# A float32 decoder trunk on one core: attention scores and causal pooling from float32r parts, the mask added by VectorE, and small matmul steps lined up

## The chip, the cores and the metric

The kernel runs on one core of a Trainium2 chip. The metric is the device time in microseconds (us) of one execution; lower is better. Beside the time, one execution is recorded by the hardware profiler; its engines are called PE (TensorE matmuls), PEld (TensorE weight loads), DVE (VectorE), ACT (ScalarE), POOL (GpSimd) and SP (SyncE, which starts the transfers here).

## The reference

Two layers over 256 tokens of width 1024. Each layer is a half-step SwiGLU, a mixer, and a second half-step SwiGLU, every one behind an RMS norm whose scale and shift come from a conditioning vector. The mixer of layer 0 is the even one, that of layer 1 the odd one.

```
def even_mixer(h, w_in, w_pool, pool_scale, lam_params, subln_g, w_out, lambda_init):
    p = h @ w_in                                  # u: 4 groups of 128; q, k: 4 heads x 2 x 64; v: 4 x 128
    y_pool = pool_mixer(u, w_pool, pool_scale)
    y_diff = diff_attention(q, k, v, lam_params, subln_g, lambda_init)
    return concatenate([y_pool, y_diff]) @ w_out

def pool_mixer(u, w_group, scale):                # group g: window w = 2, 4, 8, 16
    total = cumsum(u)[t] - cumsum(u)[t - w]
    pooled = total / min(t + 1, w) - u
    return (pooled_g @ w_group[g]) * scale

def diff_attention(...):                          # per head, c = 0 and 1
    s_c = q_c k_c^T (64 wide), causal mask, p_c = softmax(s_c / 8)
    o = rmsnorm((p_0 - lam * p_1) @ v) * subln_g * (1 - lambda_init)
```

The odd mixer is a chunkwise mLSTM with two chunks of 128 tokens and four heads: gates, a running maximum, scores, a carried state, a norm per head.

## The kernel before

Everything is kept transposed: a tile holds 128 features (partitions) by 256 tokens. A *unit* is one 128x128 block of a trunk weight against a 256-column input. Weights (`raww`) stream in chunks of 1 MB; each half chunk of 8 units is cut by ACT (L288, `wh`) and DVE (L289, `wl`) into two float32r parts whose sum is the float32 weight, and the input is likewise `xh` and `xl`. A unit is then three float32r matmuls (`mm3`, lines L330, L331, L332): wh·xh, wl·xh, wh·xl. Modulation weights (`rawm`) stream beside them; DVE reduces each half chunk in one custom instruction (L256).

What is not a unit is written as Python generators, called lanes: `head(h)` (scores, softmax, values, norm), `turn_v`, `pool_group` and, in the odd mixer, `gates`, `head_qk`, `head_v`. A lane issues its small matmuls, then yields a number of units after which it goes on. The emitted program then goes through a list scheduler, and the order of each engine is what comes out of it; each engine runs its instructions in that order. PSUM has 8 banks, each `one()` is a bank. Small float32 matmuls go to PE as two records each, float32r ones as one record.

In the first half step (`first_ffn`) the inputs of k tile 0 to 7 are made one after another: `xn[k]` (x times rstd, L518: DVE for k = 0, POOL for k = 1 to 7), `xh` (ACT L548), a second copy in float32 (ACT L549), `xl` (DVE L550), behind the modulation columns of that k (`acol`, L356). 48 matmuls (`START_BLOCKS`) use each k before the next is needed. `constants()` is written behind that loop, but its POOL instructions, which wait for nothing, are placed early by the scheduler: the four 128x384 matrices `band` (L220 to L229) by which the pooling is a matmul.

In the even mixer `head` adds the mask by a matmul (L616: identity times `masks3`, 384 columns, 128 rows) and then the product of q and k on the 64 rows of one half of the array (L618, L620, float32), for c = 0 and c = 1. `pool_group` multiplies u by `w_pool` (L686, two float32 matmuls) and the result by a band (L691, L692, L693, three). The block order is q, k, v of head 0 to 3 and then u3, u2, u1, u0, so the pooling stands at the end; `EVEN_OUT_K` is the order in which the output projection takes the eight parts of the mixer's result (0 to 3 pooling, 4 to 7 heads).

In `gates` of the odd mixer four float32 matmuls with 4 rows (L798) spread a row over the partitions, one for each head, 6 units apart.

## Time and profile before

| | |
|---|---|
| time, median of 3 runs | 1001.25 us (1001.18 to 1003.7) |
| span of the profiled execution | 1000.4 us |
| busy share PE / DVE / ACT / POOL | 97% / 79% / 53% / 19% |
| matmul instructions | 8004 |
| mean DMA rate | 247 GB/s |

The span is that of one profiled execution; the median of the runs lies 0.85 us above it. The times of matmuls overlap (one is shown as 0.28 us long where the next begins 0.12 us later), so distances between starts are to be read, not lengths. Idle time of an engine that nothing waits for costs nothing.

### The profile page before, as it was taken

How to read it: one execution, taken by the hardware profiler on the slowest of the kernel's cores; microseconds unless marked ns; L12 is line 12 of the kernel's file. 1: busy time of each engine (PE TensorE's matmuls, PEld its weight loads, DVE VectorE, ACT ScalarE, POOL GpSimd, SP SyncE). 2: the span in 40 equal slices, each digit the busy share in tenths (PEclk: the TensorE clock that was granted, in tenths of full speed). 3: DMA queues.
4: the chain of work that ended last, by engine and by line, in shares of the span. 5: the costliest groups of instructions: out<-in, count | busy, mean ns of one | idle time of the engine just before them, and what ended most of it. 6: DMA issues, size and time to landing. Idle time of an engine off the chain costs nothing.

```text
span 1000.4 us, 19729 instructions
## 1 busy us (share of the span) xinstructions
PE 973.0 (97%) x8004; PEld 959.4 (96%) x8004; DVE 788.0 (79%) x1362; ACT 527.5 (53%) x838; POOL 192.1 (19%) x219
## 2 busy tenths in 40 slices
PE   5899999999999999999999999999999999999996
PEld 3899999998999999999999999999999999999996
DVE  5889998978878888887778888787767987777452
ACT  4466444447666445544455555444767664455441
POOL 7314220010112222211122222000000122222011
PEclk9999999999999999999999999999999999999998
DMA  8888888977647667677766767777545766564531
GB/s 339 275 333 296 334 329 312 345 284 268 223 156 275 253 238 268 252 247 259 273 232 253 257 249 253 259 292 290 212 170 213 257 234 221 194 231 173 180 112 43
DMA packets 36382, 247.18 MB, mean 247 GB/s; under 512 B 4033, under 2 KB 4417, under 8 KB 7746
## 3 DMA queue, kind: packets, MB, share of 16 engines
q1 hardware_dynamic: 36290, 245.92, 67.4%
q8 instruction: 62, 1.02, 0.4%
q14 instruction: 30, 0.25, 0.1%
HBM read 244.86 MB, written 1.05 MB: 246 GB/s over the span
## 4 chain that ended last, share of the span: by engine, by line
PE 87%; DVE 5%; issue 3%; POOL 2%; ACT 2%; DMA 1%; SPq 0%; DVEq 0%; POOLq 0%; ACTq 0%
PE one L330 28%; PE one L332 28%; PE one L331 28%; DVE wl L289 2%; DMA xa<-xT 1%; DVE rawm L256 1%; ACT wh L288 1%; POOL hr L398 1%; POOL band L229 0%; DVE xl L389 0%; PE one L620 0%; PE one L618 0%; POOL band L225 0%; PE one L415 0%; PE one L407 0%
## 5 line engine op out<-in xcount | busy, mean ns | idle before, releaser
L330 PE MATMUL one<-xh,wh 128*128 128x258 f32 (+1 forms) x1728 | 491.0, 286 | 4.3 <-ACT xh L548 4.3
L332 PE MATMUL one<-xl,wh 128*128 128x258 f32 (+1 forms) x1728 | 486.6, 284 | 3.1 <-DVE xl L550 2.9
L331 PE MATMUL one<-xh,wl 128*128 128x258 f32 (+1 forms) x1728 | 485.3, 283 | 0.5 <-DVE wl L289 0.5
L288 ACT ACTIVATE wh<-raww 128x1024 fp32r<-128x1024 f32 x320 | 337.8, 1058 | 273.6 <-PE one L332 244.0
L289 DVE TENSOR_TENSOR wl<-raww,wh 128x1024 fp32r<-128x1024 f32 x320 | 393.1, 1230 | 105.2 <-ACT wh L288 100.0
L330 PEld LDWEIGHTS one<-xh,wh 128*128 128x128 f32 x1728 | 328.4, 191 | 7.6 <-ACT xh L548 4.8
L331 PEld LDWEIGHTS one<-xh,wl 128*128 128x128 f32 x1728 | 328.7, 191 | 1.1 <-DVE wl L289 0.9
L332 PEld LDWEIGHTS one<-xl,wh 128*128 128x128 f32 x1728 | 325.7, 190 | 3.8 <-DVE xl L550 3.2
L330 PE MATMUL one<-hid,wh 128*128 128x256 f32 x832 | 234.2, 282 | 0.5 <-ACT hid L563 0.5
L332 PE MATMUL one<-hid,wh 128*128 128x256 f32 x832 | 233.6, 281 | 0.0
L331 PE MATMUL one<-hid,wl 128*128 128x256 f32 x832 | 233.2, 280 | 0.0
L475 POOL TENSOR_TENSOR hid<-h,hid 128x256 fp32r<-128x256 f32 x88 | 116.0, 1319 | 379.2 <-ACT hid L474 379.2
L256 DVE CUSTOM_DVE_ANT_0 rawm<-rawm,cact 128x1024 f32<-128x1024 f32 x144 | 188.2, 1335 | 0.0
L330 PEld LDWEIGHTS one<-hid,wh 128*128 128x128 f32 x832 | 156.7, 188 | 0.8 <-ACT hid L563 0.8
L331 PEld LDWEIGHTS one<-hid,wl 128*128 128x128 f32 x832 | 157.2, 189 | 0.0
L332 PEld LDWEIGHTS one<-hid,wh 128*128 128x128 f32 x832 | 156.6, 188 | 0.2 <-DVE hid L564 0.2
L382 POOL TENSOR_TENSOR acc<-acc,sq 128x256 f32<-128x256 f32 x41 | 34.5, 841 | 270.4 <-ACT sq L378 270.2
L489 DVE TENSOR_TENSOR t<-one,rext 128x258 f32<-128x258 f32 x132 | 55.2, 421 | 30.8 <-PE one L332 30.1
L470 ACT ACTIVATE sg<-t 128x256 f32<-128x256 f32 x66 | 33.0, 504 | 34.4 <-DVE t L489 33.3
L474 ACT ACTIVATE hid<-h 128x256 fp32r<-128x256 f32 x88 | 36.7, 417 | 21.5 <-DVE h L472 21.3
L472 DVE SCALAR_TENSOR_TENSOR h<-t,sg 128x256 f32<-128x256 f32 x66 | 32.4, 491 | 6.9 <-ACT sg L470 0.6
L441 DVE SCALAR_TENSOR_TENSOR xa<-one,gcol,xa 128x256 f32<-128x256 f32 x48 | 22.3, 478 | 17.1 <-PE one L332 17.1
(211 smaller groups left out, 479.6 us busy)
## 6 DMA issues: line engine op xcount, KB each, us to landing
raww<-wst SPq DMA_DIRECT2D x152, 1024.0 KB, 4.9
rawm<-mst SPq DMA_DIRECT2D x71, 1024.0 KB, 5.0
raww<-wst SPq DMA_DIRECT2D x16, 512.0 KB, 7.0
xa<-xT SPq DMA_DIRECT2D x4, 256.0 KB, 4.0
rawm<-mst SPq DMA_DIRECT2D x2, 512.0 KB, 8.7
outT<-fin SPq DMA_DIRECT2D x3, 256.0 KB, 2.8
pk<-pack SPq DMA_DIRECT2D x1, 416.0 KB, 6.6
outT<-fin SPq DMA_DIRECT2D x2, 128.0 KB, 2.7
```

The lines of the kernel that those rows point to most:

```text
L256: nc.vector.tensor_tensor_reduce(out=ri, in0=ri, in1=cact, scale=1.0, scalar=0.0, op0=ALU.mult, op1=ALU.add, accum_out=modc[n // KT][:, n ...
L288: nc.scalar.activation(whs[i], src, AF.Copy)
L289: ins = nc.vector.tensor_tensor(out=wls[i], in0=src, in1=whs[i].bitcast(F32), op=ALU.subtract)
L330: nc.tensor.matmul(out, lhsT=wh, rhs=rh, start=start, stop=False, skip_group_check=skip)
L331: nc.tensor.matmul(out, lhsT=wl, rhs=rh, start=False, stop=False, skip_group_check=skip)
L332: nc.tensor.matmul(out, lhsT=wh, rhs=rl, start=False, stop=stop, skip_group_check=skip)
L382: eng.tensor_tensor(out=stat["acc"], in0=stat["acc"], in1=sq, op=ALU.add)
L470: nc.scalar.activation(sg, gate, AF.Silu, bias=bias_g)
L472: nc.vector.scalar_tensor_tensor(out=h, in0=up, scalar=bias_u, in1=sg, op0=ALU.add, op1=ALU.mult)
L474: nc.scalar.activation(hh[:, 0:T], h, AF.Copy)
L475: nc.gpsimd.tensor_tensor(out=hl[:, 0:T], in0=h, in1=hh[:, 0:T].bitcast(F32), op=ALU.subtract)
L489: nc.vector.tensor_tensor(out=t[:, i, :], in0=ts.pop((f, i))[:, 0:XC], in1=rext, op=ALU.mult)
```

## The change

Scores: q and k are kept as two float32r parts each; a head's scores are 12 float32r matmuls on 64 rows that take c = 0 and c = 1 in turn, and the mask is added by DVE in the instruction that finds the row maximum; the exponential reads the sum from SBUF. Pooling: the window sums are made by POOL as shifted adds (1, 2, 3 and 4 of them for windows 2, 4, 8 and 16), the mean minus the token by DVE, and one product with `w_pool` is left, as three float32r matmuls. The bands go, 16 small constants and the two parts of `w_pool` come. `meet` rounds the place of a lane's next step up to a grid of 12 units. The four L798 matmuls of the odd mixer are issued together. The pooling parts are used in another order by the output projection. Comments in code were removed, which moves line numbers (L288/L289 become L281/L282, L256 becomes L249; L330 to L332 stay).

```diff
-EVEN_OUT_K = (4, 5, 6, 3, 2, 7, 1, 0)
+EVEN_OUT_K = (4, 5, 6, 3, 2, 1, 0, 7)
...
-        for g, w in enumerate(WINDOWS):
-            nc.gpsimd.memset(band[:, g, :], 1.0 / w)
...
-                nc.gpsimd.tensor_tensor(out=m[:, 0:P], in0=m[:, 0:P], in1=ident, op=ALU.subtract)
+        for t in range(PAD):
+            nc.gpsimd.memset(icnt[:, t:t + 1], 1.0 / (t + 1))
...
+        nc.vector.tensor_copy(wph, pcol("w_pool", 0, 512))
+        nc.vector.tensor_tensor(out=wpl, in0=pcol("w_pool", 0, 512), in1=wph.bitcast(F32), op=ALU.subtract)
...
+    def meet(n):
+        to = unit_next[0] + n - grid[0]
+        return grid[0] + -(-to // grid[1]) * grid[1] - unit_next[0]
...
         def head(h):
-            yield 8
+            yield 6
...
-            for c in range(2):
-                rows = slice(64 * c, 64 * c + 64)
-                nc.tensor.matmul(pp[c][:, 0:3 * P], lhsT=identr, rhs=masks3, start=True, stop=False,
-                                 skip_group_check=True)
-                nc.tensor.matmul(pp[c][:, 0:P], lhsT=q[rows, 0:P], rhs=kk[rows, 0:P], start=False, stop=True,
-                                 skip_group_check=True)
-                nc.tensor.matmul(pp[c][:, P:3 * P], lhsT=q[rows, P:T], rhs=kk[rows, 0:T], start=False, stop=True,
-                                 skip_group_check=True)
+            for to, qs, ks in ((slice(0, P), slice(0, P), slice(0, P)), (slice(P, 3 * P), slice(P, T), slice(0, T))):
+                for j, (a, b) in enumerate(((0, 0), (1, 0), (0, 1))):
+                    for c in range(2):
+                        rows = slice(64 * c, 64 * c + 64)
+                        nc.tensor.matmul(pp[c][:, to], lhsT=q[a][rows, qs], rhs=kk[b][rows, ks], start=j == 0,
+                                         stop=j == 2, skip_group_check=True)
...
-                    nc.vector.tensor_reduce(out=mx[:, i, c:c + 1], in_=pp[c][:, cols[i]], axis=AX.X, op=ALU.max)
+                    nc.vector.tensor_tensor_reduce(
+                        out=sc[:, c, cols[i]], in0=pp[c][:, cols[i]], in1=masks3[:, cols[i]], scale=1.0, scalar=NEG,
+                        op0=ALU.add, op1=ALU.max, accum_out=mx[:, i, c:c + 1])
...
         def pool_group(g, src, bias):
...
+            while d < w:
+                n = tmp.tile([P, PAD + T], F32, tag="ps", name=nm("ps"))
+                lo = 2 * d - 1
+                nc.gpsimd.tensor_tensor(out=n[:, lo:PAD + T], in0=s[:, lo:PAD + T], in1=s[:, lo - d:PAD + T - d],
+                                        op=ALU.add)
+                s, d = n, 2 * d
             z = slot()
-            nc.scalar.activation(z[:, 0:T], pz[:, 0:T], AF.Copy)
-            yield 18
+            nc.vector.scalar_tensor_tensor(out=z[:, 0:T], in0=s[:, PAD:PAD + T], scalar=1.0 / w,
+                                           in1=u[:, PAD:PAD + T], op0=ALU.mult, op1=ALU.subtract)
+            e = z[:, 0:w - 1]
+            nc.vector.tensor_tensor(out=e, in0=s[:, PAD:PAD + w - 1], in1=icnt[:, 0:w - 1], op=ALU.mult)
+            nc.vector.tensor_tensor(out=e, in0=e, in1=u[:, PAD:PAD + w - 1], op=ALU.subtract)
+            zh, zl = slot(F32R), slot(F32R)
+            nc.scalar.activation(zh[:, 0:T], z[:, 0:T], AF.Copy)
+            nc.vector.tensor_tensor(out=zl[:, 0:T], in0=z[:, 0:T], in1=zh[:, 0:T].bitcast(F32), op=ALU.subtract)
+            yield 12 + 2 * g
             ps = one()
-            nc.tensor.matmul(ps[:, 0:P], lhsT=z[:, 0:P], rhs=band[:, g, 0:P], start=True, stop=True)
-            nc.tensor.matmul(ps[:, P:T], lhsT=z[:, 0:P], rhs=band[:, g, P:T], start=True, stop=False)
-            nc.tensor.matmul(ps[:, P:T], lhsT=z[:, P:T], rhs=band[:, g, T:3 * P], start=False, stop=True)
+            sl = slice(g * P, (g + 1) * P)
+            for j, (a, b) in enumerate(((wph, zh), (wpl, zh), (wph, zl))):
+                nc.tensor.matmul(ps[:, 0:T], lhsT=a[:, sl], rhs=b[:, 0:T], start=j == 0, stop=j == 2)
...
+            ph, pl = slot(F32R), slot(F32R)
+            nc.scalar.activation(ph[:, 0:T], src, AF.Identity, bias=bias)
+            nc.vector.scalar_tensor_tensor(out=pl[:, 0:T], in0=src, scalar=bias, in1=ph[:, 0:T].bitcast(F32),
+                                           op0=ALU.add, op1=ALU.subtract)
+            parts[blk] = (ph, pl)
...
+            pbs = [one(), one()]
             for h in range(NH):
-                pb4 = one()
-                nc.tensor.matmul(pb4[:, 0:T], lhsT=ident[0:4, h:h + 1].broadcast_to([4, P]), rhs=mr,
-                                 start=True, stop=True)
+                nc.tensor.matmul(pbs[h // 2][:, (h % 2) * T:(h % 2 + 1) * T],
+                                 lhsT=ident[0:4, h:h + 1].broadcast_to([4, P]), rhs=mr, start=True, stop=True)
```

POOL at the start, before: these are the rows around the norm's `nr` (L398) and the first of the seven `xn` adds (L518, output `hid`); the band of the last window is still ahead of them.

```order
L398 TENSOR_TENSOR nr_185<-nv_183,mhalf 128x2
L229 TENSOR_TENSOR band<-band,ident 128x128 x2
L220 MEMSET band 128x384 x2
L222 MEMSET band 128x1 x7
L225 AFFINE_SELECT band<-band 128x128
L225 AFFINE_SELECT band<-band 128x256
L227 AFFINE_SELECT band<-band 128x128
L227 AFFINE_SELECT band<-band 128x256
L229 TENSOR_TENSOR band<-band,ident 128x128 x2
```

The rows that follow are 15 memsets and the same steps for the other window, and then the L518 rows. With the change, POOL at the same place:

```order
L220 MEMSET icnt 128x1 x16
L683 MEMSET pu_3349 128x16
L683 MEMSET pu_3401 128x16
L398 TENSOR_TENSOR nr_186<-nv_184,mhalf 128x2
L518 TENSOR_TENSOR hid_194<-xa,rext 128x256
L518 TENSOR_TENSOR hid_196<-xa,rext 128x256
L518 TENSOR_TENSOR hid_198<-xa,rext 128x256
```

Between `nr` and the first L518 nothing is left. On PE, the scores of head 0 before (the names `one` are PSUM banks, `hid` are q and k):

```order
L332 MATMUL one_2797<-xl_96,wh_2707 128x258
L616 MATMUL one_2822<-masks_121,identr 128x384
L618 MATMUL one_2822<-hid_2779,hid_2775 128x128
L620 MATMUL one_2822<-hid_2779,hid_2775 128x256
L616 MATMUL one_2823<-masks_121,identr 128x384
L618 MATMUL one_2823<-hid_2779,hid_2775 128x128
L620 MATMUL one_2823<-hid_2779,hid_2775 128x256
L330 MATMUL one_2797<-xh_89,wh_2707 128x258
```

With the change, the same head on PE (L618 are now all score matmuls, the two banks are c = 0 and c = 1):

```order
L618 MATMUL one_2782<-hid_2743,hid_2738 128x128
L618 MATMUL one_2783<-hid_2743,hid_2738 128x128
L330 MATMUL one_2763<-xh_90,wh_2669 128x258
L331 MATMUL one_2763<-xh_90,wl_2670 128x258
L332 MATMUL one_2763<-xl_98,wh_2669 128x258
L618 MATMUL one_2782<-hid_2744,hid_2737 128x128
L618 MATMUL one_2783<-hid_2744,hid_2737 128x128
L618 MATMUL one_2782<-hid_2743,hid_2737 128x256
L618 MATMUL one_2783<-hid_2743,hid_2737 128x256
```

The two banks alternate, and one unit of the trunk stands in the middle; heads 1 and 2 have such a unit too. On DVE, where the last blocks of the input projection come in, the order with the change is this (L579 is the block's first step, L693 to L700 the pooling of group 3 and then 2, L282 and L249 the weight part and the modulation sum):

```order
L579 TENSOR_TENSOR ti_3465<-one_3418,rext 128x258
L249 ISA rawm_3419,mod_110<-rawm_3419,cact 128x1024
L249 ISA mod_110 128x1
L700 TENSOR_TENSOR hid_3365<-hid_3360,hid_3364 128x256
L693 SCALAR_TENSOR_TENSOR hid_3410<-ps_3408,pu_3401 128x256
L282 TENSOR_TENSOR wl_3553<-raww_3550,wh_3552 128x1024
L696 TENSOR_TENSOR hid_3410<-ps_3408,icnt 128x7
L579 TENSOR_TENSOR ti_3534<-one_3482,rext 128x258
L697 TENSOR_TENSOR hid_3410<-hid_3410,pu_3401 128x7
L282 TENSOR_TENSOR wl_3620<-raww_3550,wh_3619 128x1024
L700 TENSOR_TENSOR hid_3415<-hid_3410,hid_3414 128x256
L693 SCALAR_TENSOR_TENSOR hid_3474<-ps_3472,pu_3467 128x256
```

PE's order just behind the last block, with the change (L705 are the pooling matmuls, L330 to L332 with `hid` inputs the output projection):

```order
L332 MATMUL one_3482<-xl_98,wh_3369 128x258
L666 MATMUL one_3509<-ident,hid_3432 128x128 x2
L643 MATMUL one_3516<-ident,sc_3265 128x128 x3
L705 MATMUL one_3556<-hid_3414,wph 128x256
L705 MATMUL one_3556<-hid_3414,wpl 128x256
L705 MATMUL one_3556<-hid_3415,wph 128x256
L330 MATMUL one_3549<-hid_3215,wh_3423 128x256
L331 MATMUL one_3549<-hid_3215,wl_3424 128x256
```

`hid_3415`, the last of the pooling inputs that PE takes ahead of the output projection, is written by DVE's next to last row above.

## Rows read from the trace of the kernel before

**Rows 1.** The page's first part: busy time, share of the span and instructions of each engine.

```profile
PE 973.0 (97%) x8004; PEld 959.4 (96%) x8004; DVE 788.0 (79%) x1362; ACT 527.5 (53%) x838; POOL 192.1 (19%) x219
```

**Rows 2.** Busy time by stretch (window, its length; then busy us and count of PE, PEld, DVE, ACT, POOL; granted clock; DMA share; GB/s): the end of the even mixer's input projection.

```profile
226.00:284.00 58.00, 57.44 (x441) 52.87 (x440) 47.51 (x130) 40.77 (x111) 4.58 (x4) 1.00 0.66 245
```

**Rows 3.** PE's timeline in the first half step (start, length, engine, line, operation, xcount, [idle before <- what ended it]).

```profile
26.44 0.28 PE L332 MATMUL one<-xl,wh 128*128 128x256 f32 x1
...
27.48 0.28 PE L331 MATMUL one<-xh,wl 128*128 128x256 f32 x1
30.62 0.58 PE L332 MATMUL one<-xl,wh 128*128 128x256 f32 x1 [2.87 <-DVE xl L550]
...
33.57 0.31 PE L330 MATMUL one<-xh,wh 128*128 128x256 f32 x1
```

**Rows 4.** POOL's timeline of the same time, in the same columns.

```profile
13.39 2.63 POOL L229 TENSOR_TENSOR band<-band,ident 128x128 f32<-128x128 f32 x2
...
25.84 6.99 POOL L518 TENSOR_TENSOR hid<-xa,rext 128x256 f32<-128x256 f32 x7
```

**Rows 5.** ACT's timeline: rstd spread over the tokens (`rext`, which the adds of L518 read), and the first row that waits for such an add.

```profile
14.74 0.38 ACT L514 ACTIVATE rext<-one 128x256 f32<-128x256 f32 x1 [3.34 <-PE one L415]
...
26.60 0.60 ACT L548 ACTIVATE xh<-hid,bcol,acol 128x256 fp32r<-128x256 f32 x1 [6.28 <-POOL hid L518]
```

**Rows 6.** DVE's timeline: the modulation columns (`acol`) of k tiles 1 and 2, the parts `xl` of k tiles 1, 2 and 3, and a modulation sum between.

```profile
22.48 0.31 DVE L356 SCALAR_TENSOR_TENSOR acol<-sc,pk 128x1 f32<-128x1 f32 x1
...
29.63 0.94 DVE L550 TENSOR_TENSOR xl<-hid,xh 128x256 fp32r<-128x256 f32 x1
30.49 1.74 DVE L256 CUSTOM_DVE_ANT_0 rawm<-rawm,cact 128x1024 f32<-128x1024 f32 x1
...
34.15 0.16 DVE L356 SCALAR_TENSOR_TENSOR acol<-sc,pk 128x1 f32<-128x1 f32 x1
...
37.13 0.42 DVE L550 TENSOR_TENSOR xl<-hid,xh 128x256 fp32r<-128x256 f32 x1
...
43.05 0.42 DVE L550 TENSOR_TENSOR xl<-hid,xh 128x256 fp32r<-128x256 f32 x1
```

**Rows 7.** PE's timeline where the first blocks of the first half step are finished.

```profile
71.62 0.28 PE L330 MATMUL one<-xh,wh 128*128 128x256 f32 x1
72.14 0.39 PE L331 MATMUL one<-xh,wl 128*128 128x256 f32 x1 [0.24 <-DVE wl L289]
```

**Rows 8.** ACT's timeline just before: two loads of function tables.

```profile
66.06 1.28 ACT L603 ACT_TABLE_LOAD   x1
...
67.93 1.28 ACT L470 ACT_TABLE_LOAD   x1
```

**Rows 9.** PE's timeline at the scores of head 0, from the last trunk matmul ahead to the second one behind.

```profile
225.92 0.28 PE L332 MATMUL one<-xl,wh 128*128 128x258 f32 x1
226.04 0.34 PE L616 MATMUL one<-masks,identr 128*128 128x384 f32 x1
...
226.63 0.60 PE L620 MATMUL one<-hid,hid 64*128 64x256 f32 x2
...
228.60 0.28 PE L331 MATMUL one<-xh,wl 128*128 128x258 f32 x1
```

**Rows 10.** The weight loads of the same time, behind the scores.

```profile
228.37 0.19 PEld L330 LDWEIGHTS one<-xh,wh 128*128 128x128 f32 x1 [0.33 <-issue]
228.48 0.19 PEld L331 LDWEIGHTS one<-xh,wl 128*128 128x128 f32 x1
```

**Rows 11.** PE's timeline at the end of the even mixer's input projection: band products of two groups, the `w_pool` products of two, and a wait in the output projection.

```profile
278.66 0.39 PE L691 MATMUL one<-band,hid 128*128 128x128 f32 x2
...
280.81 0.36 PE L330 MATMUL one<-hid,wh 128*128 128x256 f32 x1
...
281.13 0.28 PE L332 MATMUL one<-hid,wh 128*128 128x256 f32 x1
281.96 0.39 PE L330 MATMUL one<-hid,wh 128*128 128x256 f32 x1 [0.54 <-ACT hid L563]
```

**Rows 12.** PE's timeline at one of the four L798 steps of the odd mixer.

```profile
720.03 0.28 PE L332 MATMUL one<-xl,wh 128*128 128x258 f32 x1
720.24 0.69 PE L798 MATMUL one<-mr,ident 4*128 4x256 f32 x2
...
721.09 0.29 PE L331 MATMUL one<-xh,wl 128*128 128x258 f32 x1
```

**Rows 13.** DVE's groups of instructions in 226 to 284 us (line, operation, shapes, xcount, then busy us, mean ns of one, idle before and its releasers).

```profile
L289 DVE TENSOR_TENSOR wl<-raww,wh 128x1024 fp32r<-128x1024 f32 x14 | 17.1, 1218 | 1.5 <-ACT wh L288 1.4
L256 DVE CUSTOM_DVE_ANT_0 rawm<-rawm,cact 128x1024 f32<-128x1024 f32 x11 | 13.1, 1215 | 0.0
L579 DVE TENSOR_TENSOR ti<-one,rext 128x258 f32<-128x258 f32 x14 | 5.9, 423 | 3.8 <-PE one L332 3.8
L627 DVE TENSOR_REDUCE mx<-one 128x1 f32<-128x256 f32 x8 | 3.2, 415 | 0.0
...
L564 DVE SCALAR_TENSOR_TENSOR hid<-one,gc,hid 128x256 fp32r<-128x256 f32 x4 | 1.9, 482 | 1.4 <-ACT hid L563 1.4
```

**Rows 14.** POOL's groups of the whole span, in the same columns.

```profile
L475 POOL TENSOR_TENSOR hid<-h,hid 128x256 fp32r<-128x256 f32 x88 | 116.0, 1319 | 379.2 <-ACT hid L474 379.2
L382 POOL TENSOR_TENSOR acc<-acc,sq 128x256 f32<-128x256 f32 x41 | 34.5, 841 | 270.4 <-ACT sq L378 270.2
```

More of the change, by code (lines that the diff above doesn't have):

```diff
@@ L176, in trunk_kernel @@
     modc = [const.tile([P, KT], F32, name=f"mod{g}") for g in range(DEPTH * NSUB * 3)]
-    masks3 = const.tile([P, 3 * P], F32R, name="masks3")
-    identr = const.tile([P, P], F32R, name="identr")
+    masks3 = const.tile([P, 3 * P], F32, name="masks3")
     maskT = const.tile([P, P], F32, name="maskT")
     tri = const.tile([P, P], F32, name="tri")
-    band = const.tile([P, len(WINDOWS), 3 * P], F32, name="band")
+    icnt = const.tile([P, PAD], F32, name="icnt")
+    wph = const.tile([P, 512], F32R, name="wph")
+    wpl = const.tile([P, 512], F32R, name="wpl")
     wgh = const.tile([P, 64], F32R, name="wgh")
@@ L205, in constants @@
     def constants():
[L206 to L207 removed]
+        nc.gpsimd.memset(masks3, 0.0)
         for i in (0, 2):
[L209 removed]
+            m = masks3[:, i * P:(i + 1) * P]
+            nc.gpsimd.affine_select(out=m, in_=m, pattern=[[-1, P]],
                                     compare_op=ALU.is_ge, fill=NEG, base=0, channel_multiplier=1)
[L211 to L212 removed]
         nc.gpsimd.memset(maskT, 0.0)
@@ L309, in tick @@
                 step(lane)
+    grid = [0, 1]
+    def meet(n):
+        to = unit_next[0] + n - grid[0]
+        return grid[0] + -(-to // grid[1]) * grid[1] - unit_next[0]
     def run_until(cond):
@@ L669, in turn_v @@
         def turn_v(i):
[L670 removed]
+            yield meet(4)
             p = parts.pop(("v", i))
@@ L676, in turn_v @@
             nc.scalar.activation(v[:, 0:T], pt[:, 0:T], AF.Copy)
-            yield 9
             vT[i] = v
         def pool_group(g, src, bias):
-            u = keep(src, bias)
-            yield 16
-            pz = one()
-            for i in range(2):
-                sl = slice(i * P, (i + 1) * P)
-                nc.tensor.matmul(pz[:, sl], lhsT=u[:, sl], rhs=pcol("w_pool", g * P, P), start=True, stop=True)
-            z = slot()
-            nc.scalar.activation(z[:, 0:T], pz[:, 0:T], AF.Copy)
@@ L689, in pool_group @@
-            yield 18
+            w = WINDOWS[g]
+            u = tmp.tile([P, PAD + T], F32, tag="pu", name=nm("pu"))
+            nc.gpsimd.memset(u[:, 0:PAD], 0.0)
+            nc.scalar.activation(u[:, PAD:PAD + T], src, AF.Identity, bias=bias)
+            s, d = u, 1
+            while d < w:
[4 more added lines that the diff above has]
+                s, d = n, 2 * d
@@ L709, in rhs @@
             return ys[k]
+        grid[:] = [unit_next[0] + 4, 12]
         in_proj(EVEN_IN_ORDER, scalars, done)
@@ L906, in rhs @@
             return ys[k]
+        grid[:] = [unit_next[0], 12]
         in_proj(ODD_IN_ORDER, lambda: spawn(gates()), done)
```

56 lines of the change are left out of this document (22 added, 34 removed).

## The prediction

> **What bounds the kernel now.** I read the busy shares first: PE is busy 97% of the span and DVE 79% [rows 1]. PE's timeline then shows what its time is made of: one trunk matmul starts 0.12 us after the other (225.92 to 226.04 in [rows 9]), and it leaves that rhythm only for small matmuls, or where an input is late. So a change gains by what it takes from PE's row of work or from PE's waits, and loses by what it makes PE wait for. Three places matter. At the start PE stands still for a vector result at 27.48 [rows 3], and the chain behind it ends on POOL, which is busy with the bands until 25.84 [rows 4]. In the even mixer the scores of a head take 2.44 us of PE (225.92 to 228.60 less two trunk steps of 0.12, [rows 9]). At the end of that mixer's input projection DVE is busy 47.51 of 58 us [rows 2]: it follows PE at 82%, and whatever is put on it there has some 10 us of room.
>
> **The change part by part.** All terms are against the profiled span of 1000.4 us; the median of the runs lies 0.85 us above it.
>
> *Start, -4.3 us.* POOL's bands go. The seven adds L518 (7.0 us, [rows 4]) can begin when `rext` is there at 15.1 [rows 5] and are done near 22, not 32.8. ACT's `xh` of k tile 1 then no longer waits 6.28 us for an add [rows 5] but for its modulation column, which was there at 22.8 [rows 6]. The adds now run beside DVE's work of 15 to 22 us; such company makes a modulation sum 1.74 us instead of 1.22 ([rows 6] against the mean of [rows 13]), so I put the column about 0.7 us later, at 23.5. From the column to the end of `xl` an undisturbed k tile takes 3.2 us (34.31 to 37.55 for k tile 2, [rows 6]), so PE gets k tile 1 at about 27 instead of 30.6. From there a k tile costs DVE and ACT 5.92 us (37.13 to 43.05, [rows 6]), which makes k tile 2 ready at 32.9 to 33.2 where it was 37.5. PE's own work on a k tile is 48 x 0.12 = 5.7, less than that, so PE follows this chain up to k tile 7 and keeps the whole shift: -4.3. Part of it is the 13 matmuls from 30.62 to 33.57 at half speed, 2.95 us instead of 1.55 [rows 3], behind the stop. Bounds: -5.3 if the column isn't late at all, -3.3 if the adds delay it by 1.7.
>
> *Table loads, -0.4 us.* The two loads of 1.28 us stand ahead of the first activations of the SwiGLU [rows 8], and PE waits 0.40 us more than a step at 71.62 [rows 7]. In the new order these activations come first. DVE gets the two parts of `w_pool` near here, about 1.2 us, so I don't count more; bounds 0 and -0.85.
>
> *Scores, -1.5 us.* 12 float32r matmuls replace 2 mask products and 4 float32 products. The trace has no float32r matmul on 64 rows. Those with 256 columns can't go faster in one queue than 0.12 each, those with 128 columns not faster than their weight load, 0.11 (228.37 to 228.48, [rows 10]): 6 x 0.12 + 6 x 0.11 = 1.37. Leaving and re-entering full height costs 0.39: the four records of an L798 step need 4 x 0.108 at full clock and take 0.82 (720.03 to 721.09 less two steps, [rows 12]). A head is 1.76, and three heads have a trunk unit in the middle, which pays the 0.39 again. 4 x 1.76 + 3 x 0.4 = 8.3 against 9.8 now: -1.5. Bounds: if the halves c = 0 and c = 1 run beside each other the 1.37 becomes 0.69, -4.2 in all; if each of the 11 changes of half within a head costs like a change of height on one side, 0.195, it is +7.1. I take no cost for a change of half and no overlap, the middle.
>
> *Pooling on PE, -2.9 us.* Two groups' bands and two groups' `w_pool` products take 2.15 us (278.66 to 280.81, [rows 11]), so four groups 4.3. Twelve float32r matmuls of 256 columns take 1.4.
>
> *Odd mixer, -1.2 us.* Four steps of L798 pay the change of height four times, now once: 3 x 0.39. PE has no other wait there that would take it back; the results come earlier for heads 1 to 3. The grid of 12 units puts other small float32 products together, but those have all 128 rows and pay no change of height; I count 0 for it, +-0.5.
>
> *DVE at the end of the even mixer, +5 us.* New on DVE: the low parts of q and k, 8 x 0.48; the mask added with the row maximum, which by the custom instruction's 1.2 us for 1024 columns costs what the reduction costs (0.42 for 256) and a read of 0.08; for each pooling group 0.48 + 0.43 and two short ones, 1.2 ([rows 13] for all of these). That is 3.9 + 1.3 + 4.8 = 10 us in a stretch with 10 to spare, and the pooling part comes at its very end, in the same few blocks. There I followed DVE's order from the first step of block u3 to the result that the output projection takes third (head 2): four weight parts (4.9), three modulation sums (3.9), three block steps (1.3), the end of head 3's softmax (1.6), three pooling groups (3.6), three parts of results (1.4) and some twenty short ones (2), about 18.7 us, and some 1.5 us of contention, since ten shifted adds of at least 0.84 us [rows 14] run on POOL. PE's row between the same points is three blocks of 24 matmuls (8.6), the output projection's first nine (1.1), and the small products: 14.8. DVE is 5.4 us behind, in waits at L705 and at the output projection's third and fifth inputs. Today's wait there is 0.7 (281.13 to 281.96, [rows 11]); the adds' own chain for window 16, 4 x 0.84 to 1.32, makes the first `z` late by a little more. Net +5. Bounds: +1 if the waits of DVE overlap as they do now, +8 if each add costs 1.3 and blocks the DVE step beside it.
>
> The Trainium skill (SBUF — State Buffer, "Who interferes with whom") has only the port pair shared by VectorE and GpSimd as a cause of contention, and as an exclusive lock. By full blocking the ten adds would cost DVE up to 8 us there rather than my 1.5; the trace's 1.74 against 1.22 is a loss of 0.5 in an instruction, less than a whole add.
>
> Sum: -4.3 - 0.4 - 1.5 - 2.9 - 1.2 + 5.0 = -5.3, a span of 995.1 and a time of 996.0.
>
> **The rivals.**
>
> *The halves overlap.* Consecutive score matmuls use different rows of the array and different banks. Then the scores gain 2.7 more: 993.3. Nothing in the trace shows two halves one behind the other (now a mask product of full height lies between them). The Trainium skill (TensorEngine Tiling (Array Packing), "Key Properties") says that different tiles can load and multiply in parallel, and that only a change of tiling mode, not of tile, drains the array. Our 0.39 at a change of height agrees with the second; for the first no row speaks.
>
> *Each change of half drains* (the other side). With a price p of a change, the scores cost 44 p more. At p = 0.12 the whole gain is gone, from 0.19 on the kernel is slower by over 3 us; at the 0.195 that a change of height costs on one side it is +8.6: 1004.6. For it speaks that every change of rows in the trace costs this; against it that none of them keeps the height.
>
> *The start gains nothing.* If DVE or the transfers, and not the adds, set when the early k tiles are ready, the 4.3 stays: 1000.3. Against it stands the named releaser in [rows 5].
>
> *DVE's end takes less or more.* At +1 the time is 992, at +8 999; only from +13 on would it be slower.
>
> **How the numbers follow.** The sum as it stands, with the end between its bounds: 0.50. Overlap 0.20. No gain at the start 0.12. Changes of half that drain 0.09; a worse end of the even mixer than +8, 0.09. 0.3% (3 us) is what a measurement can tell from no change. Faster: the first, the second and a part of the rest, 0.71; within 3 us: 0.18; slower: 0.11. The likeliest case's own range is 992 to 999. The range of 8 in 10 goes from 990 (overlap with a small end) to 1001.5 (no gain at the start with a larger end, or half of the draining).
>
> **What would show it.** In the trace after: no band on POOL, L518 from about 15 us, PE's k tile 1 without the 2.9 us wait, k tile 2 at 33; a head's scores 1.8 us (2.2 with a unit in the middle), and from their starts whether two halves begin together (overlap), 0.11 to 0.12 apart (as summed) or 0.3 apart (drain); one L798 group of 1.3 us; at 270 to 285 us waits of PE on DVE at L705 and L330 of 5 to 6 us together. I am wrong if PE has no waits there, or if the early shift is gone by 72 us.

## The result and the profile after

The changed kernel takes 1013.5 us (median of 4 runs, 1012.4 to 1013.9) where the kernel before takes 1001.5 (median of 4): a ratio of 1.0114 [1.0102, 1.0126], slower by 1.1%. The forecast was 996.0 with a range of 990 to 1001.5. The profiled execution has a span of 1012.2 us, 11.8 longer than before.

The page's first part of the changed kernel, which answers to [rows 1]:

```profile
span 1012.2 us, 19704 instructions
PE 970.5 (96%) x7984; PEld 958.6 (95%) x7984; DVE 800.2 (79%) x1402; ACT 529.2 (52%) x838; POOL 182.6 (18%) x195
```

PE has 20 instructions and 2.5 us of busy time less, and the span is longer: the time went into waits, and into stretches at half clock. Both kernels have the same 7680 trunk matmuls, in the same order but for the parts of the even mixer's output projection, so the start of the n-th in one trace can be set against the n-th of the other. The lag of the changed kernel (negative: it is earlier) is: -2.1 us at k tile 2 of the first half step (n = 96; 35.38 against 37.47), -1.4 at 78 us, +4.7 behind the even mixer (n = 2208), +4.2 ahead of the odd mixer's heads (n = 5424), +11.9 behind them (n = 6144). So the start gave 1.4, the even mixer took 6.2 and the odd mixer 7.7.

**The start.** POOL, DVE and PE of the changed kernel (start, length, ..., [idle before <- what ended it]), to be set beside [rows 3 to 6]:

```profile
13.32 1.78 POOL L398 TENSOR_TENSOR nr<-nv,mhalf 128x2 f32<-128x2 f32 x1 [9.72 <-DMA raww<-wst]
16.88 9.29 POOL L518 TENSOR_TENSOR hid<-xa,rext 128x256 f32<-128x256 f32 x7 [1.78 <-ACT rext L514]
```

```profile
13.33 1.22 DVE L249 CUSTOM_DVE_ANT_0 rawm<-rawm,cact 128x1024 f32<-128x1024 f32 x1
...
22.15 1.75 DVE L249 CUSTOM_DVE_ANT_0 rawm<-rawm,cact 128x1024 f32<-128x1024 f32 x1
...
25.51 0.68 DVE L353 TENSOR_TENSOR bcol<-mod,pk 128x1 f32<-128x1 f32 x1
...
26.30 0.16 DVE L356 SCALAR_TENSOR_TENSOR acol<-sc,pk 128x1 f32<-128x1 f32 x1
...
29.28 0.42 DVE L550 TENSOR_TENSOR xl<-hid,xh 128x256 fp32r<-128x256 f32 x1
```

```profile
29.75 0.39 PE L332 MATMUL one<-xl,wh 128*128 128x256 f32 x1 [0.30 <-DVE xl L550]
```

The 2.87 us wait of [rows 3] is 0.30 now, as forecast. But POOL's `nr` on two columns takes 1.78 us: it starts at 13.32, DVE's modulation sum at 13.33, and `nr` ends 0.6 us behind that sum's end (14.55). In the run with late bands below the order is nearly the same, and it takes 0.70:

```profile
13.26 0.70 POOL L399 TENSOR_TENSOR nr<-nv,mhalf 128x2 f32<-128x2 f32 x1 [10.28 <-DMA raww<-wst]
```

```profile
13.29 1.25 DVE L257 CUSTOM_DVE_ANT_0 rawm<-rawm,cact 128x1024 f32<-128x1024 f32 x1
```

The 17 traces of this document split in the same way. In four of them `nr` begins between 0.004 us ahead of a modulation sum and 0.04 us behind its start; there it takes 1.74 to 1.78 and ends 0.55 to 0.56 behind the sum. In the other 13 it begins 0.02 us or more ahead of the sum and takes 0.70 to 0.72.

The seven adds take 9.29 us instead of 7.0, and three of DVE's short steps take 0.68 or 0.69 instead of 0.15. The column of k tile 1 is there at 26.46, not 23.5. Some 0.6 us of this isn't the change's: `nr` starts at 13.32 where it started at 12.72 before, and over the 17 traces, whatever the kernel, it starts at 11.76 to 13.32.

**The end of the even mixer.** ACT, DVE and PE, where before there was one wait of 0.54 us [rows 11]:

```profile
273.81 0.42 ACT L699 ACTIVATE hid<-hid 128x256 fp32r<-128x256 f32 x1 [2.37 <-DVE hid L697]
...
277.34 1.06 ACT L281 ACTIVATE wh<-raww 128x1024 fp32r<-128x1024 f32 x1 [2.63 <-PE one L332]
278.69 0.42 ACT L699 ACTIVATE hid<-hid 128x256 fp32r<-128x256 f32 x1 [0.29 <-DVE hid L697]
...
279.41 0.26 ACT L657 ACTIVATE hid<-one 128x128 f32<-128x128 f32 x1
...
281.80 0.63 ACT L661 ACTIVATE hid<-one,hr 128x128 f32<-128x128 f32 x2 [1.78 <-POOL hr L398]
```

```profile
273.19 0.59 DVE L697 TENSOR_TENSOR hid<-hid,pu 128x15 f32<-128x15 f32 x1
...
280.83 0.15 DVE L396 TENSOR_SCALAR hv<-ss 128x2 f32<-128x2 f32 x1
```

```profile
274.28 0.39 PE L705 MATMUL one<-hid,wph 128*128 128x256 f32 x1 [2.39 <-ACT hid L699]
...
282.22 0.73 PE L666 MATMUL one<-ident,hid 128*128 128x128 f32 x2 [4.91 <-ACT hid L661]
```

The longest wait of PE isn't for a pooling product. L666 transposes the result of head 2, whose values PE had finished at 267.4. Its squares (L657) stand on ACT behind two pooling parts (L699), each waiting for DVE, and run at 279.4. They stand behind a weight part (L281) too, which waits 2.63 us for PE's own matmuls, so a delay of PE comes back to it through ACT. The clock falls behind the first wait (columns as in [rows 2], 4 us each):

```profile
270.00:274.00 4.00, 1.89 (x16) 1.67 (x15) 3.97 (x7) 1.26 (x2) 2.54 (x3) 1.00 0.31 68
274.00:278.00 4.00, 3.03 (x14) 2.73 (x14) 4.00 (x8) 1.37 (x3) 1.67 (x3) 0.59 0.84 307
278.00:282.00 4.00, 0.00 (x0) 0.00 (x0) 4.00 (x22) 1.93 (x8) 2.08 (x4) 0.50 0.71 231
282.00:286.00 4.00, 3.78 (x21) 3.67 (x22) 3.08 (x21) 2.73 (x8) 0.00 (x0) 0.63 0.49 207
```

From about 274.8 to 285 the granted clock is at half: trunk matmuls there start 0.215 us apart instead of 0.12. DVE is busy without a gap from 270 to 282, while PE is busy for 4.9 of these 12 us.

**The scores.** Head 3 on PE, to be set beside [rows 9] (x8 are eight matmuls in one row):

```profile
256.68 0.44 PE L618 MATMUL one<-hid,hid 64*128 64x128 f32 x4
257.49 0.73 PE L618 MATMUL one<-hid,hid 64*128 64x128 f32 x8 [0.37 <-DVE hid L719]
258.15 0.39 PE L330 MATMUL one<-xh,wh 128*128 128x258 f32 x1
258.38 0.28 PE L331 MATMUL one<-xh,wl 128*128 128x258 f32 x1
```

The single records start in pairs: 256.682 and 256.686, 256.846 and 256.849, 257.492 and 257.495, 257.657 and 257.661, 257.829 and 257.832, 257.946 and 257.949. The two halves of the array work beside each other, at 0.12 to 0.17 us a pair where none waits. Counted as in the prediction (and with head 0's end taken like the others', since a transpose follows it), the four heads take 2.05, 1.86, 1.82 and 1.66 us, 7.4 in all, with 1.6 of waiting for low parts in them; before it was 4 x 2.44 = 9.8.

**The odd mixer.** PE's waits there (us in total, times, longest); before it had 1.2 us in all:

```profile
PE one L890 <- ACT hid L885: 3.3, 1, 3.3
PE one L865 <- ACT hid L846: 1.5, 2, 1.0
PE one L844 <- DVE hid L842: 0.9, 3, 0.5
PE one L865 <- ACT dr L876: 0.3, 1, 0.3
```

The longest is at the other end from the first heads: L890 transposes the result of the last head, and between trunk matmuls 5900 and 5920 the lag grows from 6.9 to 12.3.

```profile
786.92 0.48 PE L890 MATMUL one<-ident,hid 128*128 128x128 f32 x1 [3.27 <-ACT hid L885]
```

The scale that this head's squares (L880, ACT) need is ready on DVE at 777.05; they run at 782.50, behind steps of other blocks.

### The profile page after: what moved, and what is told of

Its sections match the earlier page's. It is cut to its first block, busy times and chain, and to the rows that moved or that the text cites. A ratio compares the mean times of both kernels' runs of the same rounds, so it can differ in the third digit from the quotient of the medians.

```text
span 1012.2 us, 19704 instructions
## 1 busy us (share of the span) xinstructions
PE 970.5 (96%) x7984; PEld 958.6 (95%) x7984; DVE 800.2 (79%) x1402; ACT 529.2 (52%) x838; POOL 182.6 (18%) x195
## 4 chain that ended last, share of the span: by engine, by line
PE 85%; DVE 6%; issue 4%; ACT 3%; POOL 1%; DMA 1%; SPq 1%; DVEq 0%; ACTq 0%; POOLq 0%
PE one L330 28%; PE one L332 27%; PE one L331 27%; DVE wl L282 2%; DVE rawm L249 1%; ACT wh L281 1%; DMA raww<-wst 1%; DVE xl L389 1%; PE one L415 0%; POOL ps L689 0%; POOL hr L398 0%; ACT sc L631 0%; DVE sc L625 0%; DVE ti L579 0%; POOL nr L398 0%
## 5 line engine op out<-in xcount | busy, mean ns | idle before, releaser
L330 PE MATMUL one<-xh,wh 128*128 128x258 f32 (+1 forms) x1728 | 489.7, 285 | 4.5 <-ACT xh L548 4.5
L332 PE MATMUL one<-xl,wh 128*128 128x258 f32 (+1 forms) x1728 | 486.6, 284 | 0.6 <-DVE xl L550 0.5
L281 ACT ACTIVATE wh<-raww 128x1024 fp32r<-128x1024 f32 x320 | 337.6, 1058 | 280.9 <-PE one L332 253.3
L282 DVE TENSOR_TENSOR wl<-raww,wh 128x1024 fp32r<-128x1024 f32 x320 | 395.6, 1239 | 104.7 <-ACT wh L281 99.5
L330 PEld LDWEIGHTS one<-xh,wh 128*128 128x128 f32 x1728 | 328.8, 191 | 5.6 <-ACT xh L548 4.8
L332 PEld LDWEIGHTS one<-xl,wh 128*128 128x128 f32 x1728 | 325.8, 190 | 1.5 <-DVE xl L550 1.0
L330 PE MATMUL one<-hid,wh 128*128 128x256 f32 x832 | 234.7, 282 | 0.0
L332 PE MATMUL one<-hid,wh 128*128 128x256 f32 x832 | 233.4, 281 | 0.0
L249 DVE CUSTOM_DVE_ANT_0 rawm<-rawm,cact 128x1024 f32<-128x1024 f32 x144 | 187.0, 1325 | 0.0
L330 PEld LDWEIGHTS one<-hid,wh 128*128 128x128 f32 x832 | 157.6, 189 | 0.4 <-ACT hid L563 0.4
L332 PEld LDWEIGHTS one<-hid,wh 128*128 128x128 f32 x832 | 157.1, 189 | 0.0
```

Of the source, the lines that this page charges most:

```text
L249: nc.vector.tensor_tensor_reduce(out=ri, in0=ri, in1=cact, scale=1.0, scalar=0.0, op0=ALU.mult, op1=ALU.add, accum_out=modc[n // KT][:, n ...
L281: nc.scalar.activation(whs[i], src, AF.Copy)
L282: ins = nc.vector.tensor_tensor(out=wls[i], in0=src, in1=whs[i].bitcast(F32), op=ALU.subtract)
L330: nc.tensor.matmul(out, lhsT=wh, rhs=rh, start=start, stop=False, skip_group_check=skip)
L332: nc.tensor.matmul(out, lhsT=wh, rhs=rl, start=False, stop=stop, skip_group_check=skip)
```

## Experiments

Changes of single stages below are lags of trunk matmuls, as above, against the profiled execution of before. A time without an interval is that of one execution; those of the kernel before lie between 1000.8 and 1003.9, so such a time alone settles no difference of 1 or 2 us. Lags vary too: three runs with one and the same even mixer (the changed kernel and the next two) lose 6.2, 6.9 and 7.2 us in it.

**The odd mixer as before.** `odd_mixer` taken from the kernel before.

```diff
-            yield meet(14)
+            yield 14
...
-            pbs = [one(), one()]
             for h in range(NH):
+                pb4 = one()
...
+                yield 6
```

> The changed kernel with the odd mixer written as before (no grid, four L798 steps 6 units apart). By the two traces the odd mixer of the changed kernel loses 7.9 us against that of before. Theory A, the loss sits in the odd mixer's own code: about 1005.6 us. Rival, the odd mixer only passes on a delay that comes from the start or the even mixer: about 1013, no change.

1006.3 us against 1002.3 (ratio 1.0043 [1.0028, 1.0058]). The lag is the same at the odd mixer's begin and end (+4.2): theory A holds, the rival is out.

**No grid in the odd mixer.**

```diff
-        grid[:] = [unit_next[0], 12]
+        grid[:] = [unit_next[0], 1]
```

> The changed kernel with the odd mixer's grid of 12 units set to 1, the four L798 products still issued together. Theory A1, the rounding makes the gates late (their last step is at 729.5 us, 9 us later against the stream than before) and then bunches the heads: 6 of the 7.9 us come back, about 1007.5, and what is left is the half clock behind the eight 4-row matmul records. Rival A2, issuing the L798 together costs it: about 1012 to 1013.

1014.5: nothing comes back, and A1 falls. The odd mixer now loses 9.0, and the waits have moved: 4.3 us at the first heads' products (L844), with half clock behind them, and none at L890. So the grid by itself isn't the cause. It may be what puts a wait at L890: the run with the old pooling below, which has the grid, has it too (3.3), and no run without the grid has it.

**The grouping alone,** in the kernel before.

```diff
+            pbs = [one(), one()]
             for h in range(NH):
-                pb4 = one()
-                nc.tensor.matmul(pb4[:, 0:T], ...)
+                nc.tensor.matmul(pbs[h // 2][:, (h % 2) * T:(h % 2 + 1) * T], ...)
+            for h in range(NH):
...
-                yield 6
```

> The kernel before with the four L798 products issued together (two PSUM tiles, no yield of 6 units between heads) and nothing else changed. The run without the grid kept the odd mixer's loss (a wait of some 6 us at the first heads' products), so the grid alone isn't it. Theory D, the grouping is: the 8 subtractions on DVE and 12 exponentials on ACT of all four heads now stand in one piece ahead of head 0's products in both queues, and PE waits for these: 4 to 8 us slower than before, 1005 to 1010. Rival, the other shifted steps (units to wait in head_qk and head_v) make it: 1000, a gain of the 1.2 us of changes of height.

1009.8, 7.6 over the runs of before on that chip. In the trace 6.8 of it is lost in the odd mixer, all at the first heads, and 0.7 was there from the start. PE, DVE and ACT of this run:

```profile
717.53 1.97 PE L798 MATMUL one<-mr,ident 4*128 4x256 f32 x8
720.25 0.61 PE L821 MATMUL one<-hid,hid 128*128 128x128 f32 x4
...
728.41 0.37 PE L825 MATMUL one<-ident,hid 128*128 128x128 f32 x1 [4.13 <-DVE hid L823]
```

```profile
726.79 1.23 DVE L289 TENSOR_TENSOR wl<-raww,wh 128x1024 fp32r<-128x1024 f32 x1 [0.46 <-ACT wh L288]
727.93 0.42 DVE L823 SCALAR_TENSOR_TENSOR hid<-one,hid 128x256 f32<-128x256 f32 x1
```

```profile
725.71 1.05 ACT L288 ACTIVATE wh<-raww 128x1024 fp32r<-128x1024 f32 x1
726.65 0.69 ACT L806 ACTIVATE hid<-hid,col 128x128 f32<-128x128 f32 x2
727.23 0.36 ACT L807 ACTIVATE hid<-one,mc 128x128 f32<-128x128 f32 x1
```

The score product of the first head (L821) stands at 720.25, right behind the group; before it came at 729.84. ACT's last factor for the heads ends at 727.6, where before it ended at 728.3: ACT and DVE work no faster. The four yields of 6 units were not only places for a small matmul, they were the 24 units (8.6 us) that ACT and DVE worked in. On PE itself the saving is there: the group takes some 2.0 us, where the four steps took 3.2.

**The grouping, and the 24 units put back behind it.**

```diff
                 st["dw"][h], st["qw"][h] = dw, qw
+            yield 24
```

> The kernel before with the four L798 products issued together and then a yield of 24 units, the four yields of 6 put behind them. Theory D2, the grouping lost 7.7 us because the four yields of 6 were also the time in which ACT and DVE made the four heads' factors: without them the first heads' products stand 24 units earlier in PE's order and wait. With the units back the waits go and the changes of height are saved: 1000.0 to 1001. Rival, the eight DVE and twelve ACT steps in one piece hold the weight parts and PE waits anyway: 1003 or more.

1003.35 beside 1002.15. The time is the rival's, but the waits are gone (1.5 us in the whole odd mixer, 1.2 before), which supports D2. The odd mixer still loses 1.1, since PE's clock falls behind the group. This run in stretches of 2 us:

```profile
717.00:719.00 2.00, 2.00 (x12) 1.48 (x11) 2.00 (x6) 0.00 (x0) 0.00 (x0) 0.94 0.45 111
719.00:721.00 2.00, 2.00 (x9) 1.82 (x9) 1.17 (x9) 0.71 (x1) 0.00 (x0) 0.50 1.02 430
721.00:723.00 2.00, 2.00 (x14) 2.00 (x13) 1.23 (x2) 1.97 (x5) 0.00 (x0) 0.71 1.01 422
723.00:725.00 2.00, 2.00 (x19) 2.00 (x18) 1.33 (x7) 2.00 (x7) 0.00 (x0) 1.00 0.21 86
```

PE didn't wait ahead of it; it ran the 4-row matmuls for 2.3 us. In the changed kernel the same happened from 732 to 735, and in the run with the old pooling; in two other runs with the group it did not.

**The pooling of before** in the changed kernel: `pool_group`, the bands and their POOL work taken from before.

```diff
-            for j, (a, b) in enumerate(((wph, zh), (wpl, zh), (wph, zl))):
-                nc.tensor.matmul(ps[:, 0:T], lhsT=a[:, sl], rhs=b[:, 0:T], start=j == 0, stop=j == 2)
+            nc.tensor.matmul(ps[:, 0:P], lhsT=z[:, 0:P], rhs=band[:, g, 0:P], start=True, stop=True)
...
```

> The changed kernel with the pooling of before (bands, w_pool in float32) and nothing else undone. Theory B, the late vector chain of the new pooling makes PE wait 8 us at 270 to 285 and the half clock behind it: these go, 2.9 us of PE work and some 1.4 us at the start come back: even mixer some 7 us shorter, 1008 in all. Rival, the grid or the scores make the even mixer's loss: waits stay, 1014 to 1017.

1009.3. The even mixer is 0.6 us under that of before (lag +0.2 to -0.4): the new pooling costs some 6.8 there, theory B's size. How it does so took four more runs.

**The pooling blocks earlier,** with the odd mixer of before, no grid in the even mixer, and the output projection's order changed to fit.

```diff
-EVEN_IN_ORDER = _blocks("q0 k0 v0 q1 k1 v1 q2 k2 v2 q3 k3 v3 u3 u2 u1 u0")
+EVEN_IN_ORDER = _blocks("q0 k0 v0 q1 k1 v1 q2 k2 u3 u2 q3 k3 u1 u0 v2 v3")
...
-EVEN_OUT_K = (4, 5, 6, 3, 2, 1, 0, 7)
+EVEN_OUT_K = (4, 5, 3, 2, 1, 0, 6, 7)
...
-        grid[:] = [unit_next[0] + 4, 12]
+        grid[:] = [unit_next[0] + 4, 1]
```

> The changed kernel with the odd mixer of before, no grid in the even one, and the pooling blocks moved ahead: the order of blocks is q0 k0 v0 q1 k1 v1 q2 k2 u3 u2 q3 k3 u1 u0 v2 v3, so that no pooling group stands behind the last block. Theory B, the loss of 6.6 us by the new pooling is its place at the end, where ACT and DVE hold the heads' results behind it: PE's waits there go and the even mixer comes 2 to 4 us under that of before, 995 to 998. Rival, DVE has no room for it at any place in this mixer: waits of about the same size further ahead, 1002 to 1006.

1005.7, an even mixer 6.6 longer than before: the rival. PE waits 5.8 us at L705 in five places.

**The same run, with a later place for the pooling matmuls.**

```diff
-            yield 12 + 2 * g
+            yield 40
```

> The run with the pooling blocks moved ahead, and 40 units between a pooling group's vector work and its matmuls on PE instead of 12 to 18. There PE's matmuls L705 waited 5.8 us in all and the half clock came behind these waits, wherever the blocks stood. Theory B2, as in the odd mixer the matmuls stand too early in PE's order, ahead of what ACT, DVE and POOL can have ready: the waits go, the even mixer is 2 to 4 us under that of before, 996 to 999. Rival, DVE and ACT are full there and the wait moves to the scores or the heads' results: 1003 to 1006.

1007.0, and the even mixer loses 8.3: the rival again, and worse. L705 waits no more, but L666 does, 9.0 us in two places, for the result of a head that stands behind a weight part and a pooling step on ACT and behind further steps on DVE.

**The shifted adds on DVE,** blocks at the end, odd mixer of before.

```diff
-                nc.gpsimd.tensor_tensor(out=n[:, lo:PAD + T], ...)
+                nc.vector.tensor_tensor(out=n[:, lo:PAD + T], ...)
```

> The changed kernel with the odd mixer of before, and the ten shifted adds of the pooling on DVE instead of POOL. DVE gets some 4 us of work more, but a pooling group goes from ACT to DVE and on without POOL between. Theory B3, the loss of 6.5 us in the even mixer is made of waits from engine to engine, in which POOL's adds and DVE's two-input steps also hold each other up (POOL's add 2.41 us instead of 0.65, DVE's short step 0.54 instead of 0.15): at least 3 us come back, 1002 to 1003.5. Rival, DVE is full and any work on it at this place comes out of PE: 4 us more, 1009 to 1011.

1005.0; the even mixer's loss is 5.9 instead of 6.9, which is hardly outside the 6.2 to 7.2 of the runs above. Both expectations miss. The adds are 4.3 us on DVE, but DVE's busy time from 224 to 290 us is only 1.2 longer (57.3 against 56.1), and PE loses nothing by it. Taking POOL out gave back 1.0 at most. PE still waits 6.7 us at L666.

**The last two vector steps of a group later in the queues,** odd mixer of before.

```diff
+            yield 10
             zh, zl = slot(F32R), slot(F32R)
...
-            yield 12 + 2 * g
+            yield 8
```

> The changed kernel with the odd mixer of before, and each pooling group's last two vector steps (L699 on ACT, L700 on DVE) written 10 units later, the matmuls 8 behind. With that ACT takes head 2's squares (L657) ahead of the pooling parts instead of behind two of them. In the run without this change L657 had its input at 267 us and ran at 279; PE then waited 5.3 us at that head's result (L666) and 0.5 of the clock came with it. Theory B4, the wait is that place in ACT's queue: the waits at L666 and L705 fall from 9.0 to under 3 us in all and the even mixer's loss of 6.9 to 1 or less, about 1000. Rival, DVE is too full and PE waits elsewhere as much: 1004 to 1007.

1002.15, between the two expectations; the loss is 3.7 instead of 6.9. PE's waits at L666 and the pooling products fall from 9.0 to 5.3 us, and head 2's squares run at 269.4, not 279.4. So nearly half of the loss goes with the order of ACT's queue. That it is the squares' place alone is likely, not shown, since the edit moves the steps of all four groups. The two longest waits of PE that are left:

```profile
272.36 0.39 PE L706 MATMUL one<-hid,wph 128*128 128x256 f32 x1 [1.91 <-ACT hid L700]
...
275.61 0.47 PE L666 MATMUL one<-ident,hid 128*128 128x128 f32 x1 [2.39 <-ACT hid L661]
```

```profile
273.55 1.60 POOL L398 TENSOR_TENSOR hr<-hv,mhalf 128x2 f32<-128x2 f32 x1 [0.98 <-DVE hv L396]
```

The first waits for the pooling's own chain. The second waits for `hr`, whose input stands in DVE's queue, and 0.9 us of it is `hr` itself: it begins 0.17 us behind a modulation sum and takes 1.60 instead of the 0.70 that it took in the changed kernel (281.06). What of the rest is DVE's load and what order stays open.

**The new scores alone,** in the kernel before: `head` and `done` of the changed kernel with the steps of before (8, 28, 12, 12).

> The kernel before with the new scores alone (q and k in two parts, mask added by DVE), without grid and with the old pooling and start. In the changed kernel's trace two score matmuls on different halves begin 2 to 3 ns apart, six pairs in 1.15 us, where a head took 2.44. Theory C: 4 x 1.2 us less, with waits for the low parts of up to 1.6 in all: 996.5 to 998.5. Rival: the eight low parts and the masks on DVE make PE wait as much as is won: 1001.

1000.3 against 1002.3, ratio 0.9984 [0.9975, 0.9994]. The lag falls by 2.4 in the even mixer. A head takes 1.09 to 1.91 us instead of 2.44; the shortest, head 3, has no wait in it. The time is nearer to the rival than to theory C: two heads wait for low parts (0.9 us), a head's result (L663) 0.6, and the output projection 0.9 at its begin.

**Three matmuls on one half, then three on the other,** in that kernel.

```diff
-                for j, (a, b) in enumerate(((0, 0), (1, 0), (0, 1))):
-                    for c in range(2):
+                for c in range(2):
+                    for j, (a, b) in enumerate(((0, 0), (1, 0), (0, 1))):
```

> The kernel before with the new scores alone, c outermost: three matmuls on one half of the array, then three on the other, with the 128-column part first and the 256-column part behind it. Theory C, it is the overlap of two halves in turn that makes a head 1.1 to 1.3 us: without it the starts lie 0.11 to 0.12 apart, 0.5 to 0.7 us more for a head, 2 to 3 us in all against the run with scores alone: 1002 to 1003. Rival, the array takes the two halves beside each other in any order: no change, 1000.3.

1000.2, the even mixer gains 2.3 as against 2.4, and the shortest head still takes 1.09: the rival. In that head all starts are in pairs again (245.672 and 245.682, 245.835 and 245.848), though three matmuls of one half stand ahead of the other's in the order: it looks as if each half takes its own next matmul. In two of the other heads, where a low part comes late for one half, only some starts are in pairs, and they take 1.39 and 1.65.

**The pooling and odd mixer of before, and no grid in the even mixer.**

> The changed kernel with the pooling and the odd mixer of before and the even mixer's grid set to 1: left of the change are the new scores with their shifted steps, the order of the output projection and the new constants, with the bands at the start. With the grid the same even mixer gained 0.6 us, the scores put in by themselves 2.3. Theory G, the grid's rounding costs these 1.7 us: even mixer 2 to 2.5 us under that of before, 1000 to 1001. Rival, it is the other steps (6 units instead of 8 ahead of the scores) or the order of the projection: 1001.5 to 1002.5.

1001.7 beside 1002.5. The even mixer is 0.7 us under before, where with the grid it was 0.6: theory G falls, the rival holds. PE waits 1.5 us for q and k parts behind the shorter step of 6 units and 1.1 behind the shorter one of `turn_v`; the grid itself is worth no more than some 0.2 here.

**Bands right behind the adds,** in the kernel before: their code in a block that queues it on POOL behind the last L518.

> The kernel before with POOL's bands built behind the seven adds of xn, nothing else changed: the start of the changed kernel by itself. In the three runs with the changed start so far, k tile 2 begins 2.1, 3.1 and 4.2 us earlier, and 0.7 us is lost again by 78 us. Theory E, that is kept: 2 to 3.5 us faster, 998 to 999.5. Rival, the bands collide with DVE later instead (they run beside the k tiles 3 to 6) and the gain is lost there: 1001.

1001.0 against 1002.2, ratio 0.9987 [0.9978, 0.9997]. k tile 2 starts 3.0 earlier, but by 78 us the lag is -0.6: POOL is busy to 48 us, where DVE and ACT set the pace, and a k tile there takes longer than its 5.92 (the columns of k tiles 1, 2 and 3 come at 25.32, 32.15 and 38.79). The rival, nearly.

**Late bands and new scores together.**

> The kernel before with the new scores and the late bands, and with the pooling, the odd mixer and the steps of before. Theories C and E add up: 2 (scores alone) and 2 to 3.5 (start): 996 to 998. Rival, the start's gain is lost: 999.5 to 1000.5.

998.95, ratio 0.9965 [0.9951, 0.9979]: the two gains add.

**Bands behind the last four hidden blocks of the first half step, and new scores.**

```diff
+        swiglus[0] += 1
+        if NF - 4 < swiglus[0] <= NF:
+            with tc.issue_after(ins.ins):
+                make_band(swiglus[0] - NF + 3)
```

> The kernel before with the new scores, and with each band built by POOL behind one of the last four hidden blocks of the first half step (near 150 us) instead of the first 40 us. The run with the bands right behind the adds lost 2.4 of its 3.0 us again by 78 us, while DVE and ACT set the pace of the k tiles and POOL's bands ran beside them. Theory E2, bands put where DVE has a lead cost nothing: 2 from the scores and 3 from the start, 996 to 997.5. Rival, the start's gain is lost by 78 us without bands too: 998.5 to 999.5.

996.6 against 1002.2, ratio 0.9942 [0.9925, 0.9958]: faster than both kernels, by 0.6% than before and by some 1.7% than the changed kernel, which ran on another chip. The start's 2.3 us at 78 us are kept and the scores add 2.4. The PE line of its page:

```profile
span 995.7 us, 19766 instructions
PE 966.6 (97%) x8012; PEld 955.2 (96%) x8012; DVE 792.4 (80%) x1384; ACT 527.9 (53%) x838; POOL 199.1 (20%) x219
```

## Why the prediction was wrong

Of the 17.1 us between the forecast span (995.1) and the measured one, the odd mixer makes 8.9, the even mixer 5.6 and the start with the table loads 3.3; 0.7 came back elsewhere.

- **The start, -4.3: right in mechanism, too large.** The wait for the adds goes. The step that failed is "about 0.7 us later": the column of k tile 1 came at 26.46, not 23.5. `nr` behind a DVE sum cost 1.1, this execution began 0.6 later, and seven two-input steps of DVE were stretched beside the adds, six of them by some 0.53. In ten runs with this start k tile 2 came 2.1 to 4.2 us earlier; counted from the start of `nr`, 2.7 to 3.8. The Trainium skill (SBUF — State Buffer, "Who interferes with whom") says that the port pair shared by VectorE and GpSimd is an exclusive lock, that a VectorE instruction with two SBUF inputs contends with a GpSimd instruction that reads SBUF, and that the order of issue decides which of them is blocked. `nr`'s end 0.56 behind the sum in four traces agrees with that, and so does a POOL add of 2.41 us that begins beside three DVE steps in a row, where others of its size take 0.63. The other side isn't seen with `nr`: where it came first, the sum behind it took 1.21 to 1.25, so DVE wasn't held for `nr`'s 0.70. I had set the rule aside because one DVE step loses only 0.5; by these rows a POOL step that comes second loses more.
- **Table loads, -0.4: wrong, +0.7.** The first activations came earlier, but the weight part behind them, at 68.28, now stands behind four of them instead of two. PE waits 0.92 at 70.69 in the changed kernel, and the lag grows from -2.2 to -1.4 here.
- **Scores, -1.5: two errors against each other.** The four heads take 7.4 us of PE, 0.9 less than the 8.3 of the sum. The overlap that I gave 0.20 is there (-2.7), and the wait for low parts that I didn't count (1.6) takes more than half of it back. The price for leaving full height came from a misread row: an L798 step is two records of 0.216, not four of 0.108, which makes the same 0.43. The drain at a change of half, the rival on the other side, is out: pairs start 1 to 9 ns apart. The Trainium skill (TensorEngine Tiling (Array Packing), "Key Properties") says that different tiles can load and multiply in parallel; these starts bear that out.
- **Pooling on PE, -2.9: not measured by itself.** That 3.4 us come back between n = 1968 and 2016, where the bands stood, agrees with it.
- **DVE at the end of the even mixer, +5: too small.** With the pooling and scores terms I had +0.6 for this mixer, and it was +6.2. The step that failed is the walk along DVE alone. It found DVE 5.4 us behind, and DVE is indeed without a gap there. But the long wait goes from DVE to ACT's queue, and there a head's step stands behind pooling steps that it has nothing to do with: I had named L705 and L330, and PE waited 2.4 at L705, nothing at L330 and 5.8 at L666. Waits of 8.2 us and the clock at half behind them move the lag by 9.6 between n = 1920 and 1968.
- **Odd mixer, -1.2: wrong, +7.7, the largest error (8.9).** The sentence that failed is "PE has no other wait there that would take it back": PE waits 6.0 us there. I costed the yields of 6 units at nothing, as if only PE's instructions were moved; they covered 8.6 us of ACT and DVE work. The grouping alone lost 6.8 by that, and 9.0 in the changed kernel without the grid. That the changed kernel's 7.7 comes from this mixer's own code is shown by the run with the old odd mixer. How it divides is not shown: with the grid, the heads' products (L844 and L865) wait 2.7 us, the half clock from 732 to 735 costs some 2, and the last head's transpose waits 3.3, which it does in no run without the grid. So the 0 that I counted for the grid has no support either, and a run with the grid and the four steps apart, which would tell, is missing.
- **The rival for a slower kernel** had the wrong place: it was draining, with 0.09. A worse end of the even mixer than +8 was in the list; a loss in the odd mixer was not.

## What to carry to other kernels

Units between two steps of a small chain are time for other engines, not only a place for its matmul: who groups the matmuls must put the units back behind the group. Here that took the waits away, but the half clock behind the group ate the gain. When vector work is added to an engine that runs its steps in order, look for steps of other chains that will stand behind it: here PE lost 8.2 us in waits and ran at half clock for 10 us behind some 4 us of added work, and nearly half of the loss went when two of the added steps of each group were queued later. Work that is needed only some 250 us later (the bands) belongs where the engine that it slows has a lead, not where it is merely ready.

## What the runs showed of the hardware

- Two 64-row matmuls on the two halves of the array start 1 to 9 ns apart where the halves alternate, and 10 to 16 ns in a head where three of one half stand ahead in the order; six matmuls of 128 columns and six of 256 take 1.09 us with entry and exit.
- About 2.3 us of 4-row matmuls without a wait were followed by half clock at once in three of five runs with such a group; in the changed kernel that cost some 2 us.
- A POOL step on 2 columns took 1.74 to 1.78 us in four traces where it began from 0.004 us ahead of a two-input DVE step to 0.04 us behind its start, and 0.70 to 0.72 in 13 where it began 0.02 us or more ahead; the DVE step took 1.21 to 1.25 in all of them.
